# Convolution with 2x2 max pool on one core: the differences of four steps made in two halves, and all instructions in a new order

## The chip, the core and the metric

The kernel runs on one core of a Trainium2 chip. A core has five engines that work at the same time, each through its own queue of instructions: TensorE (PE: matmuls; its weight loads are shown apart as PEld), VectorE (DVE), ScalarE (ACT), GpSimd (POOL) and SyncE (SP, which here only issues transfers). Matmuls write into PSUM, a memory of eight banks. The metric is the time of one execution on the device in microseconds; lower is better.

## The reference: what is computed

A 3x3 convolution with padding 1 over 16 images of 64 channels and 64x64 points, to 128 channels, and then the maximum over every 2x2 square:

```python
x_pad = np.pad(x, ((0, 0), (0, 0), (pad, pad), (pad, pad)))
conv[b, co] += weight[co, ci, kh, kw] * x_pad[b, ci, kh:kh+h, kw:kw+w]    # over ci, kh, kw
output[b, c, i, j] = np.max(conv[b, c, 2*i:2*i+2, 2*j:2*j+2])
```

Input, weights and output are fp32: x is 16 x 64 x 64 x 64, the weights are 128 x 64 x 3 x 3, the output is 16 x 128 x 32 x 32.

## The kernel before, in words

Two images lie side by side on the 128 partitions (64 channels each); a matmul of one image uses 64 rows of TensorE's array, so that those of the two images ("lane" 0 and 1) can run beside each other. The work is cut into 32 steps: 8 pairs of images times 4 quarters, each quarter 8 output rows, that is 16 rows of the convolution. For each step and lane two PSUM banks are built: A and B stand for the two rows of the convolution under each output row. The larger of both, and then of neighbouring columns, is the output.

There are two kinds of steps, in the sequence `SEQ`. A **K step** (8 of them) multiplies the bf16 rows `kx` themselves. A **W step** (24 of them) first forms sums and differences of fp32 rows `wx` and so needs four products of three taps instead of six for two rows of the convolution. With x0 to x3 for the four rows that an output row needs:

- `E` (tile `we`): x1 - x2, and `S` (tile `ws`): x1 + x2, 512 elements per partition each;
- `V` (tile `wv`): differences of rows two apart, 1024 elements: its even rows serve bank A, its odd rows bank B. Step 1 makes the two halves apart, `Ve` (even rows) and `Vo` (odd rows), into tiles `vh` of 512 elements (`rv_half`).

The products of a W step are P2 (E times the weights GM, begins bank A), P0 (even half of V, into A), P3 (odd half of V, into B) and P1 (S times GP, into B). Those of a K step are PAa and PAb into A, PBa and PBb into B, and PR with `KS`, the sum of two rows of `kx`. Products of both lanes that stand next to each other in the order are issued tap by tap in turn. Around the products stand, for each step `s` and lane `l`:

- `SE.s.l` (`seed`, on ScalarE, L439) or `SEv.s.l` (on VectorE, L437): copies A, with P2 alone in it, to bank B. It comes between P2 and P0, and P0 and P3 wait for it. Where bank B held transposed weights, `seed` first issues a matmul of zeros into it;
- `EV` (ScalarE, L423 and L425): copies A out to the tile `ev`; `MX` (VectorE, L443): maximum of B and `ev`, into B. P1 or PR, which is common to both rows, is added behind it;
- `OD` (ScalarE, L466) copies the odd columns, `CM` (VectorE, L475) takes the maximum with the even ones, `ST` stores two lanes of a step. With `CM` the bank is free for another step.

`CP` (ScalarE, L290) lifts the row x1 into a PSUM bank for some steps, and `E` and `S` on VectorE then read it there (L294). All other row operations on VectorE and POOL go through `row_op` (L196). There a POOL operation is made to wait for the last VectorE row operation, or cast by VectorE (L193), that stands ahead of it in the order; lifted E and S do not count:

```python
inst = eng[e].tensor_tensor(out=out, in0=in0, in1=in1, op=op)
if e == "g":
    behind(inst, last_row[0])
else:
    last_row[0] = inst
```

Loads: `LX` (SP's queue) brings a chunk of `wx`, or of the fp32 `kf` of steps 0 and 2, which `XO` and `XE` cast to odd and even rows of `kx`; `LK` (POOL's queue) loads `kx` with a cast on the way. A load waits for the outputs of the step 12 (W) or 13 (K) ahead of it. At the start the weights are combined (`c.`), transposed on TensorE into PSUM banks (`T.`) and copied out (`TV.`, L240 to L244).

The order of all this is written out by hand, as a list of tokens in `ORDER`: each engine executes its own tokens in the order of the list. `:v`, `:a` and `:g` say VectorE, ScalarE and POOL; a number says a PSUM bank; a letter behind the lane (`1a`) means half of the rows. Tiles come from pools with a fixed number of buffers, in the order of the list: 8 for each of `ks`, `ws` and `we`, 6 for `wv`, 4 for `vh`.

Of the kernel before, what the change touches and what calls it, by code (L numbers as in the profile page):

```python
# [20 lines left out]
PAa.0.1b PAa.0.0b EV.1.0 MX.1.1 E.3:v PAb.0.0a PAb.0.1a MX.1.0 PBb.0.1a PBa.0.0b PAb.0.1b PAb.0.0b  # L21
XE.2:a S.3:v PBa.0.1b PBb.0.0a XO.2:a EV.0.0 P2.3.0:5 P1.1.1 KS.0:v EV.0.1 SE.3.0:2 E.4:v OD.1.1
PBb.0.0b PBb.0.1b LX.6 PAa.2.1:0 P1.1.0 OD.1.0 MX.0.1 LK.5 MX.0.0 P0.3.0 PBa.2.1:3 EV.3.0 P3.3.0
PR.0.1 LX.7 OD.0.1 CM.1.1 CM.1.0 LK.9 PAb.2.1 PR.0.0 LX.8 CP.6:5 P2.3.1:7 PAa.2.0:6 MX.3.0 CM.0.1
PBb.2.1 P1.3.0 V.4:g EV.2.1 SE.3.1:4 E.6:v OD.0.0 S.6:v PAb.2.0 P2.4.1:0 P2.4.0:5 P3.3.1 S.4:g
KS.2:v OD.3.0 LX.10 CM.3.0 LX.11 EV.2.0 SE.4.1:6 CM.0.0 PBa.2.0:2 P0.3.1 LX.13 LX.12 E.7:g PBb.2.0
P0.4.1 MX.2.1 SE.4.0:1 P0.4.0 PR.2.1 V.6:v EV.3.1 MX.2.0 P2.6.1:7 P3.4.0 EV.4.1 PR.2.0 P3.4.1 MX.3.1
EV.4.0 OD.2.1 LK.14 MX.4.0 V.7:g SE.6.1:5 CM.2.1 PAa.5.0:0 P1.3.1 OD.2.0 OD.3.1 CM.2.0 MX.4.1 P1.4.0
P0.6.1 P3.6.1 PBa.5.0:3 CM.3.1 PAb.5.0 PAa.5.1:2 OD.4.0 P1.4.1 P2.6.0:4 EV.6.1 V.10:g CM.4.0 PAb.5.1
PBb.5.0 CP.8:1 S.7:g EV.5.0 MX.6.1 OD.4.1 E.8:v S.8:v P2.7.0:7 P1.6.1 SE.6.0:0 EV.5.1 OD.6.1 CM.4.1  # L30
SE.7.0:6 PBa.5.1:1 P0.6.0 MX.5.0 EV.6.0 E.10:g P3.6.0 P2.7.1:2 CM.6.1 KS.5:v P0.7.0 PBb.5.1 SE.7.1:5
EV.7.0 PR.5.0 P2.10.1:4 S.10:v P0.7.1 P3.7.0 OD.5.0 MX.6.0 MX.5.1 SE.10.1:7 LX.16 CM.5.0 P1.6.0
P3.7.1 MX.7.0 PR.5.1 PAa.9.0:3 EV.7.1 OD.6.0 V.8:g LX.15 OD.5.1 CM.6.0 P2.8.0:2 P0.10.1 MX.7.1
CM.5.1 PAb.9.0 P3.10.1 CP.11:0 E.11:v ST.0 P1.7.1 P1.7.0 EV.10.1 SE.8.0:1 EV.9.0 S.11:v V.13:g
OD.7.1 P0.8.0 P2.8.1:4 ST.4 OD.7.0 MX.10.1 ST.6 CM.7.1 P2.10.0:3 PAa.9.1:0 P3.8.0 P1.10.1 CM.7.0
EV.8.0 SE.8.1:5 SE.10.0:2 PAb.9.1 PAa.14.0:6 OD.10.1 E.12:g P0.8.1 P0.10.0 V.11:v KS.9:v EV.9.1
EV.8.1 P3.10.0 P3.8.1 EV.10.0 CM.10.1 PAa.14.1:0 PAb.14.0 MX.8.0 MX.8.1 ST.2 LX.17 PBa.9.0:7
PBa.9.1:4 ST.5 MX.10.0 PAb.14.1 P1.8.0 V.12:g ST.3 CP.13:3 E.13:v EV.14.0 P2.11.1:6 P1.10.0 LK.18
KS.14:v OD.8.0 EV.14.1 PBb.9.0 P1.8.1 S.13:v V.16:g OD.10.0 P2.11.0:0 PBb.9.1 SE.11.1:3 OD.8.1
# [44 lines left out]
def kernel(  # L84
# [9 lines left out]
    BF16 = mybir.dt.bfloat16  # L94
    MAX = mybir.AluOpType.max
    ADD = mybir.AluOpType.add
    SUB = mybir.AluOpType.subtract

    B, CI, H, W = x.shape
# [229 lines left out]
        t = row["E", s] = row_pool.tile([128, R, W], BF16, name="we")  # L329
        two_rows(s, t, e, SUB)  # L330

    def rv(s, e):
# [36 lines left out]
    def pw(block, name, first, stride=1, at=0):  # L369
        def of(s, l, part):  # L370
            half = (name + "eo"[at], s)
            t, n, f = (row[half], 1, 0) if half in row else (row[name, s], stride, at)
            i0, i1 = PARTS[part]
            return (
                block, i0, i1,
                lambda lo, c0, c1: t[lo : lo + CI, f + n * i0 : n * i1 : n, c0:c1],
                first,
            )

        return of  # L380
# [135 lines left out]
    for token in ORDER.split():  # L516
# [29 lines left out]
            lift(int(args[0]), int(at))  # L546
        elif name in ("XO", "XE"):
            to_bf16(int(args[0].rstrip("ab")), args[0].lstrip("0123456789"), int(name == "XO"), at)
        elif name in ("KS", "S", "E", "V"):
            f = rs_cast if name == "S" and int(args[0]) in ADDED else None  # L550
            (f or {"KS": ks, "S": rs, "E": re, "V": rv}[name])(int(args[0]), at)
# [54 lines left out]
```

## Time and profile before

| | |
|---|---|
| median of 3 runs | 104.32 us (103.85 to 105.15) |
| the profiled execution | 103.82 us, of which the span is 102.1 us |
| busy TensorE, VectorE, ScalarE, POOL | 95.8, 91.3, 89.4, 80.2 us |
| read from and written to HBM | 17.07 MB and 8.39 MB, 249 GB/s over the span |

The span runs from the first instruction to the last that the profiler recorded; the rest of the execution's time, 1.7 us, lies around it. A row of the groups reads: line, engine, operation, output tile, input tiles, shapes, count, busy us, mean ns of one, and the idle time of the engine just ahead with what ended it. A row of the timeline begins with its start and its length in us; several equal instructions in a row are one row with a count, and its length is then from the first start to the last end.

### The profile page before, as it was taken

How to read it: one execution, taken by the hardware profiler on the slowest of the kernel's cores; microseconds unless marked ns; L12 is line 12 of the kernel's file. 1: busy time of each engine (PE TensorE's matmuls, PEld its weight loads, DVE VectorE, ACT ScalarE, POOL GpSimd, SP SyncE). 2: the span in 40 equal slices, each digit the busy share in tenths (PEclk: the TensorE clock that was granted, in tenths of full speed). 3: DMA queues.
4: the chain of work that ended last, by engine and by line, in shares of the span. 5: the costliest groups of instructions: out<-in, count | busy, mean ns of one | idle time of the engine just before them, and what ended most of it. 6: DMA issues, size and time to landing. Idle time of an engine off the chain costs nothing.

```text
span 102.1 us, 2473 instructions
## 1 busy us (share of the span) xinstructions
PE 95.8 (94%) x869; PEld 56.0 (55%) x869; DVE 91.3 (89%) x178; ACT 89.4 (88%) x199; POOL 80.2 (79%) x63
## 2 busy tenths in 40 slices
PE   6968999999999999999999999999999999999940
PEld 2335844677785466444787655555555555564610
DVE  0599999999999999999989998699998999988980
ACT  5589989979989998999899988999998987999830
POOL 7006997799699397999899999998698999999000
PEclk9999999999999999999999999999999999999995
DMA  2999999993279999567897999968998505302353
GB/s 64 307 265 417 424 409 326 302 345 70 84 171 387 303 348 358 108 87 175 185 361 196 305 310 367 307 233 180 334 371 291 206 6 206 103 12 94 116 198 103
DMA packets 13789, 24.07 MB, mean 236 GB/s; under 512 B 1104, under 2 KB 9680, under 8 KB 13776
## 3 DMA queue, kind: packets, MB, share of 16 engines
q1 hardware_dynamic: 12624, 22.16, 65.3%
q0 software_dynamic: 864, 1.56, 8.9%
q10 hardware_dynamic: 288, 0.20, 0.6%
q8 instruction: 7, 0.11, 0.5%
q14 instruction: 6, 0.05, 0.1%
HBM read 17.07 MB, written 8.39 MB: 249 GB/s over the span
## 4 chain that ended last, share of the span: by engine, by line
PE 86%; DVE 5%; DMA 4%; ACT 1%; issue 0%; SPq 0%; DVEq 0%
PE acc L408 86%; DMA wx<-in_x_dram 4%; DVE o L475 1%; DVE acc L443 1%; DVE we L196 1%; ACT od L466 1%; DVE acc L437 1%; DVE vh L196 1%; DVE wq L196 1%; SPq L536 0%; DVE o L485 0%; DVE ws L196 0%; DVEq L443 0%
## 5 line engine op out<-in xcount | busy, mean ns | idle before, releaser
L408 PEld LDWEIGHTS <-wt 64*128 64x128 bf16 x840 | 53.8, 94 | 37.6 <-ACT acc L439 2.6
L408 PE MATMUL acc<-wv,wt 64*128 64x504 bf16 (+1 forms) x276 | 58.5, 377 | 0.0
L196 POOL TENSOR_TENSOR wv<-wx 128x1024 bf16<-128x1024 f32 x21 | 49.4, 2359 | 5.5 <-DVE ks L196 2.1
L443 DVE TENSOR_TENSOR acc<-acc,ev 128x512 f32<-128x512 f32 x64 | 43.2, 692 | 2.8 <-ACT ev L423 1.9
L408 PE MATMUL acc<-kx,wt 64*128 64x504 bf16 (+5 forms) x216 | 38.2, 350 | 0.0
L408 PE MATMUL acc<-we,wt 64*128 64x512 bf16 (+1 forms) x144 | 36.6, 377 | 1.0 <-ACT wt L240 0.9
L408 PE MATMUL acc<-ws,wt 64*128 64x512 bf16 (+1 forms) x144 | 34.6, 377 | 0.2 <-DVE acc L443 0.2
L423 ACT ACTIVATE ev<-acc 128x512 f32<-128x512 f32 x48 | 28.8, 608 | 1.2 <-PE acc L408 0.9
L439 ACT COPY acc<-acc 128x512 f32<-128x512 f32 x46 | 27.2, 595 | 1.4 <-DVE o L475 0.4
L475 DVE TENSOR_TENSOR o<-acc,od 128x256 f32<-128x256 f32 x64 | 25.4, 414 | 1.7 <-ACT od L466 0.9
L466 ACT COPY od<-acc 128x256 f32<-128x256 f32 x64 | 23.4, 382 | 3.2 <-PE acc L408 1.9
L196 POOL TENSOR_TENSOR we<-wx 128x512 bf16<-128x512 f32 x11 | 14.0, 1268 | 2.1 <-PE acc L408 1.4
L408 PE MATMUL acc<-ks,wt 64*128 64x504 bf16 (+1 forms) x48 | 12.4, 376 | 0.0
L196 POOL TENSOR_TENSOR ws<-wx 128x512 bf16<-128x512 f32 x9 | 11.4, 1266 | 0.4 <-DVE ks L196 0.4
L425 ACT COPY ev<-acc 128x512 f32<-128x512 f32 x16 | 9.3, 589 | 1.2 <-PE acc L408 1.1
L294 DVE TENSOR_TENSOR we<-acc,wx 128x512 bf16<-128x512 f32 x11 | 7.5, 682 | 0.0
L294 DVE TENSOR_TENSOR ws<-acc,wx 128x512 bf16<-128x512 f32 x11 | 7.5, 681 | 0.0
L290 ACT COPY acc<-wx 128x512 f32<-128x512 f32 x11 | 6.6, 599 | 0.1
L196 POOL TENSOR_TENSOR vh<-wx 128x512 bf16<-128x512 f32 x1 | 1.3, 1277 | 5.2 <-DVE vh L196 5.2
L503 PE MATMUL acc<-const-bfloat16-1.0 128*128 128x512 bf16 x8 | 3.6, 627 | 0.8 <-PEq L587 0.8
L196 DVE TENSOR_TENSOR gsum<-wraw 128x192 f32<-128x192 f32 x1 | 0.5, 502 | 3.6 <-DMA wraw<-in_weight_dram 3.6
L275 POOL DMA_DIRECT2D kx<-in_x_dram x6 | 3.5, 586 | 0.2 <-issue 0.2
(29 smaller groups left out, 32.1 us busy)
## 6 DMA issues: line engine op xcount, KB each, us to landing
out_dram<-o SPq DMA_DIRECT2D x30, 256.0 KB, 6.0
wx<-in_x_dram SPq DMA_DIRECT2D x12, 512.0 KB, 6.8
wx<-in_x_dram SPq DMA_DIRECT2D x6, 544.0 KB, 6.0
wx<-in_x_dram SPq DMA_DIRECT2D x6, 480.0 KB, 7.9
kx<-in_x_dram POOLq DMA_DIRECT2D x3, 256.0 KB, 5.3
kf<-in_x_dram SPq DMA_DIRECT2D x1, 512.0 KB, 7.8
kx<-in_x_dram POOLq DMA_DIRECT2D x2, 240.0 KB, 8.7
wraw<-in_weight_dram SPq DMA_DIRECT2D x1, 288.0 KB, 2.8
```

Source lines behind the costliest of these rows:

```text
L196: inst = eng[e].tensor_tensor(out=out, in0=in0, in1=in1, op=op)
L275: paced(s, nc.gpsimd.dma_start(out=kx_of(p)[:, lo:hi, :], in_=rows_of(p, lo, hi)))
L290: nc.scalar.copy(out=acc[bank], in_=wrow(s, 0))
L294: nc.vector.tensor_tensor(out=t, in0=lifted[s], in1=wrow(s, 1), op=op)
L408: yield lambda kw=kw, o0=o0, o1=o1, c0=c0, c1=c1: nc.tensor.matmul(acc[t][:, i0:i1, o0:o1], wt[l * CI : l * CI + CI, K * BLOCKS[block] + T ...
L423: inst = nc.scalar.mul(t, acc[bank["A", s, l]], -1.0)
L425: inst = nc.scalar.copy(out=t, in_=acc[bank["A", s, l]])
L439: nc.scalar.copy(out=acc[b], in_=acc[bank["A", s, l]])
L443: nc.vector.tensor_tensor(out=t, in0=t, in1=ev[s, l], op=MAX)
L466: nc.scalar.copy(out=od[s, l][:, i0:i1], in_=acc[bank["B", s, l]][:, i0:i1, 1::2])
L475: done[s, l] = nc.vector.tensor_tensor(out=outs(s)[:, l, i0:i1], in0=acc[bank["B", s, l]][:, i0:i1, 0::2], in1=od[s, l][:, i0:i1], op=MAX,)
L503: nc.tensor.matmul(acc[n], ones[:, 0:128], ones, start=True, stop=True, skip_group_check=True)
```

## The change

Steps 3, 4, 30 and 31 make their V in two halves, `Ve` and `Vo`, into two tiles `vh`, as step 1 did, instead of one `wv`. Their even halves are on POOL; the odd half of step 3 is on VectorE, the others on POOL. So P0 of these steps can begin when the even half is there, and P3 when the odd half is.

The whole list `ORDER` is replaced, with other banks, and some operations change their engine:

- VectorE no longer has E.4, TV.D2, TV.GP, SEv.1.1, SEv.31.1 and V.11. It has E.7, S.16, Vo.1, Vo.3, XO.0a, XO.0b, SEv.21.1, SEv.25.0 and SEv.31.0 in addition.
- POOL no longer has E.7, S.16, Vo.1 and the four whole V; it has E.4, V.11 and seven halves.
- ScalarE no longer has SE.21.1, SE.25.0, SE.31.0, XO.0a and XO.0b; it has SE.1.1, SE.31.1, TV.D2 and TV.GP.
- SE.1.1 now goes to bank 2, which held transposed weights, so that `seed` issues one matmul of zeros.
- Loads and stores stand in another order: LX.8 ahead of LX.7, LX.13 behind LX.16 and LX.15, LK.5 ahead of the first row operation of POOL.

The beginning, from before and after:

```diff
-LW c.g1:a LX.1 LX.0a T.G1:0 c.GS:v c.g0:a c.D0:v c.GM:v T.D0:1 c.D2:v T.G0:2 c.g2:a T.GM:3 E.1:v
-c.GP:v Ve.1:v TV.GM:a P2.1.1:4 P2.1.0:5 TV.D0:a TV.G1:a TV.G0:a SE.1.0:6 SEv.1.1:7 T.D2:3 T.GP:1
-T.G2:0 P0.1.1 P0.1.0 TV.G2:v Vo.1:g LX.0b XE.0a:a LX.3 XO.0a:a TV.D2:v LX.2 P3.1.1 P3.1.0 S.1:v
-XO.0b:a XE.0b:a V.3:g EV.1.1 LX.4 CP.3:0 TV.GP:v PAa.0.0a:2 PAa.0.1a:3 PBa.0.1a:4 PBa.0.0a:1
...
+LW c.GS:v c.D2:v c.GM:v c.g1:a T.G1:0 T.D2:1 LX.1 c.D0:v c.g2:a E.1:v c.g0:a T.GM:2 TV.G1:a c.GP:v
+T.G0:3 Ve.1:v T.D0:4 LX.0a TV.GM:a TV.G0:a TV.D0:a P2.1.1:5 P2.1.0:6 TV.D2:a SE.1.0:7 XO.0a:v T.G2:0
+TV.G2:v SE.1.1:2 T.GP:3 Vo.1:v LX.0b PAa.0.1a:4 PAa.0.0a:1 XE.0a:a P0.1.0 P0.1.1 XO.0b:v S.1:v
+PBa.0.0a:0 PAb.0.1a LX.3 P3.1.1 P3.1.0 TV.GP:a XE.0b:a LX.2 LX.4 PBa.0.0b PBa.0.1a:3 LX.6 EV.1.0
+LK.5 PAb.0.0a PAa.0.1b EV.1.1 PBb.0.0a PBb.0.1a Vo.3:v KS.0:v MX.1.0 CP.3:6 PBa.0.1b PAa.0.0b Ve.3:g
...
```

The order of VectorE's and POOL's tokens around the places that the prediction names, in the new list (other engines left out):

```
VectorE: XO.0a TV.G2 Vo.1 XO.0b S.1 Vo.3 KS.0 MX.1.0 MX.1.1 E.3 S.3 MX.0.1 MX.0.0 CM.1.0 CM.1.1 E.6 S.6 KS.2
         CM.0.1 CM.0.0 MX.2.1 V.6 MX.2.0 MX.3.1 MX.3.0 CM.2.1 CM.2.0 MX.4.0 CM.3.1 CM.3.0 E.7 MX.4.1 ...
POOL:    LK.5 Ve.3 E.4 S.4 Ve.4 Vo.4 LK.9 LK.14 S.7 V.7 V.10 E.10 V.8 V.11 LK.18 E.12 V.12 E.15 V.13 V.15 E.16
         LK.23 V.16 S.15 E.19 V.17 S.19 V.22 LK.27 V.19 E.21 V.20 V.21 S.21 E.24 V.24 E.26 V.25 V.26 E.29 S.26
         S.29 V.28 V.29 Ve.30 Ve.31 Vo.30 E.31 Vo.31 S.31
```

Six lines of code are new: a token `E.<step>a` or `E.<step>b` for half of the rows of an E, which the new list does not use, and `first and part != "b"` for it in `pw`. Behind them all line numbers are 6 higher (matmuls L408 become L414, `MX` L443 becomes L449).

More of the change, by code (lines that the diff above doesn't have):

```diff
@@ L22 @@
[L22 to L27, printed above, removed]
@@ L330, in re, with re_half @@
         two_rows(s, t, e, SUB)
+    def re_half(s, part, e):
+        if part == "a":
+            row["E", s] = row_pool.tile([128, R, W], BF16, name="we")
+        i0, i1 = PARTS[part]
+        row_op(e, row["E", s][:, i0:i1], wrow(s, 0)[:, i0:i1], wrow(s, 1)[:, i0:i1], SUB)
     def rv(s, e):
@@ L376, in of @@
                 lambda lo, c0, c1: t[lo : lo + CI, f + n * i0 : n * i1 : n, c0:c1],
-                first,
+                first and part != "b",
             )
@@ L548 @@
             to_bf16(int(args[0].rstrip("ab")), args[0].lstrip("0123456789"), int(name == "XO"), at)
+        elif name == "E" and not args[0].isdigit():
+            re_half(int(args[0][:-1]), args[0][-1], at)
         elif name in ("KS", "S", "E", "V"):
```

111 lines of the change are left out of this document (58 added, 53 removed).

## The prediction

> **What bounds the kernel now.** I read the page first (busy shares, chain), then the chain in order of time, then the timeline.
>
> ```profile
> span 102.1 us, 2473 instructions
> ...
> PE 95.8 (94%) x869; PEld 56.0 (55%) x869; DVE 91.3 (89%) x178; ACT 89.4 (88%) x199; POOL 80.2 (79%) x63
> ...
> PE acc L408 86%; DMA wx<-in_x_dram 4%; DVE o L475 1%; DVE acc L443 1%; DVE we L196 1%; ACT od L466 1%; DVE acc L437 1%; DVE vh L196 1%; DVE wq L196 1%; SPq L536 0%; DVE o L485 0%; DVE ws L196 0%; DVEq L443 0%
> ```
>
> TensorE is the bound: 86% of the chain that ended last is its matmuls. But VectorE and ScalarE, at 89% and 88% busy, are close behind. The chain in order of time (start us, length us, what) says where TensorE was held up:
>
> ```profile
> 8.20 24.43 PE acc L408 x246
> ...
> 43.14 0.29 DVE ws L196
> ...
> 43.82 52.16 PE acc L408 x471
> ...
> 96.07 0.71 DVE acc L443
> ```
>
> After 8.20 us the chain leaves TensorE for VectorE's operations at 43.1 and again at the end. To make a scale of this I need the price of TensorE's unit of work. A product (three taps) of one lane runs beside one of the other lane; three such pairs start at 14.16, 14.81 and 15.46, and the last product of the kernel at 97.42:
>
> ```profile
> 14.16 0.38 PE L408 MATMUL acc<-wv,wt 64*128 64x512 bf16 x1
> ...
> 14.81 0.38 PE L408 MATMUL acc<-kx,wt 64*128 64x512 bf16 x1
> ...
> 15.46 0.38 PE L408 MATMUL acc<-we,wt 64*128 64x512 bf16 x1
> ...
> 21.45 0.38 PE L408 MATMUL acc<-ws,wt 64*128 64x512 bf16 x1
> ...
> 97.42 0.31 PEld L408 LDWEIGHTS <-wt 64*128 64x128 bf16 x2 [0.28 <-issue]
> ```
>
> A pair costs 0.65 us. Both orders hold 136 pairs (840 matmuls). From 8.20 to 97.42 lie 134 of them, 134 x 0.65 = 87.1 us, in 89.2 us. **All that TensorE loses to waits after its start is 2.1 us**: some 0.8 of it around the last products, 1.3 spread before. A new order can win little more than that, and the end stays: in both orders P0.31, EV.31, MX.31 and P1.31 hang on each other in this way with only P1.30 beside them. Two products of one lane follow each other at 79 places before and 69 after, of little weight.
>
> Which engine is nearest to holding TensorE up (busy us of PE, PEld, DVE, ACT, POOL in 8 us; then clock, DMA):
>
> ```profile
> 16.00:24.00 8.00, 8.00 (x77) 5.04 (x73) 8.00 (x17) 7.22 (x17) 6.58 (x5) 1.00 1.02 294
> ...
> 64.00:72.00 8.00, 8.00 (x78) 4.09 (x74) 6.89 (x15) 7.97 (x20) 6.99 (x4) 1.00 0.83 235
> ```
>
> From 16 to 24 us VectorE has no idle time; from 64 to 72 it has 1.1 us. What the change puts on VectorE early is what can cost. The granted clock is full.
>
> **The change, part by part.** VectorE's prices, from start to start:
>
> ```profile
> 11.67 0.68 DVE L294 TENSOR_TENSOR ws<-acc,wx 128x512 bf16<-128x512 f32 x1
> 12.26 0.41 DVE L196 TENSOR_TENSOR ks<-kx 128x512 bf16<-128x512 bf16 x1
> 12.60 0.68 DVE L196 TENSOR_TENSOR we<-wx 128x512 bf16<-128x512 f32 x1
> 13.20 1.29 DVE L443 TENSOR_TENSOR acc<-acc,ev 128x512 f32<-128x512 f32 x2
> 14.40 0.74 DVE L475 TENSOR_TENSOR o<-acc,od 128x256 f32<-128x256 f32 x2
> ...
> 18.81 1.25 DVE L196 TENSOR_TENSOR wv<-wx 128x1024 bf16<-128x1024 f32 x1
> 19.99 1.88 DVE L443 TENSOR_TENSOR acc<-acc,ev 128x512 f32<-128x512 f32 x3
> ```
>
> That is 0.60 for 512 elements in fp32, 0.34 for a KS or a CM, 1.18 for a V. POOL's:
>
> ```profile
> L196 POOL TENSOR_TENSOR wv<-wx 128x1024 bf16<-128x1024 f32 x21 | 49.4, 2359 | 5.5 <-DVE ks L196 2.1 <-DVE ws L196 1.2 <-DMA wx<-in_x_dram 0.8
> ...
> L196 POOL TENSOR_TENSOR we<-wx 128x512 bf16<-128x512 f32 x11 | 14.0, 1268 | 2.1 <-PE acc L408 1.4 <-DVE ks L196 0.8
> ...
> L275 POOL DMA_DIRECT2D kx<-in_x_dram x6 | 3.5, 586 | 0.2 <-issue 0.2
> ```
>
> *Splitting.* Two halves on POOL, priced like the we, cost 2 x 1.27 = 2.54 for 2.36: 0.18 more for each of steps 4, 30 and 31. Step 3's odd half goes to VectorE.
>
> *Balance of engines.* VectorE gives up E.4, the weight copies TV.D2 and TV.GP, the seeds SEv.1.1 and SEv.31.1 and V.11 (0.60 + 0.6 + 1.2 + 1.18 = 3.6). It takes E.7, S.16, Vo.1, Vo.3, three seeds (21.1, 25.0, 31.0) and the two casts XO.0 (4 x 0.60 + 1.8 + 0.67 = 4.9): **+1.3 us**. Such a cast is on no row of VectorE. The nearest rows are the CM of 0.34, with as many elements, and the ws of 0.86 at 8.58 (below); I take the CM's, and a gain below it is not excluded. POOL gives up E.7, S.16, Vo.1 and four V (3 x 1.27 + 4 x 2.36 = 13.2) and takes E.4, V.11 and seven halves (8 x 1.27 + 2.36 = 12.5): -0.7. ScalarE drops three seeds and two casts for two seeds and two weight copies: about -0.4.
>
> [...]
>
> *The start.*
>
> ```profile
> 5.71 0.69 DVE L196 TENSOR_TENSOR we<-wx 128x512 bf16<-128x512 f32 x1
> ...
> 6.46 0.82 PE L408 MATMUL acc<-we,wt 64*128 64x512 bf16 x6 [0.90 <-ACT wt L240]
> ...
> 6.85 0.69 DVE L196 TENSOR_TENSOR vh<-wx 128x512 bf16<-128x512 f32 x1
> ...
> 7.33 0.57 ACT L439 COPY acc<-acc 128x512 f32<-128x512 f32 x1
> ...
> 7.62 1.28 POOL L196 TENSOR_TENSOR vh<-wx 128x512 bf16<-128x512 f32 x1 [5.19 <-DVE vh L196]
> 7.82 1.37 ACT L191 CAST kx<-kf 128x320 bf16<-128x320 f32 x4
> ...
> 8.58 0.86 DVE L196 TENSOR_TENSOR ws<-wx 128x512 bf16<-128x512 f32 x1
> ...
> 9.59 2.40 PE L408 MATMUL acc<-kx,wt 64*128 64x256 bf16 x42
> ```
>
> P2.1 begins at 6.46, right behind E.1 (5.71 + 0.69), which stays fifth on VectorE: no change. Then ScalarE makes both seeds: the second from 7.82 to 8.39, so P0.1 of lane 1 begins at 8.44 instead of 8.20 (+0.24). Ahead of it TensorE now does a half pair of step 0 (six matmuls, 6 x 2.40/42 = 0.34): its rows are cast from 7.45 to 7.8 and it runs from 7.95 to 8.29, inside that wait. Net **-0.1**. With a cast of 0.86 the cover is gone and 0.4 is lost instead. The seed of 1.1 now meets a bank that held transposes, which adds a matmul of zeros; at the 0.38 of a 512-column matmul, or at nearly twice that, it lies in the same wait.
>
> *The first third.* VectorE's own queue, from Ve.1 at 6.85 to the end of MX.3.1: 15 instructions of 0.60 (Ve.1, Vo.1, S.1, Vo.3, E.3, S.3, E.6, S.6, seven MX; S.1 without the stretch of the 0.86, since POOL is then idle), six of 0.335 (two XO, four CM), two KS, TV.G2 for 0.3, V.6 for 1.18: 9.0 + 2.0 + 0.7 + 0.3 + 1.2 = 13.2. That ends at 20.0, and 0.1 later its result is out. TensorE wants it for P1.3.1, 17.4 pairs behind P0.1: 8.44 + 17.4 x 0.65 = 19.75. So it **waits 0.35**. In the old order the product at 21.45 stands 20 pairs behind 8.20, due at 21.2: 0.25 lost by then. The difference is +0.1 if VectorE never idles. Behind MX.3.1 stand MX.3.0 and two CM, wanted just as early; I add 0.1.
>
> *The middle.* A row operation of VectorE and one of POOL do not run side by side:
>
> ```profile
> 41.62 1.26 POOL L196 TENSOR_TENSOR we<-wx 128x512 bf16<-128x512 f32 x1
> ...
> 42.49 0.94 DVE L196 TENSOR_TENSOR ws<-wx 128x512 bf16<-128x512 f32 x1
> ...
> 43.61 2.35 POOL L196 TENSOR_TENSOR wv<-wx 128x1024 bf16<-128x1024 f32 x1 [0.21 <-DVE ws L196]
> ```
>
> This ws took 0.94 instead of 0.68, and POOL's we ended at 42.88, between; it is the piece at 43.14 in the chain. The 0.86 at 8.58 is the same beside POOL's vh, which ended at 8.90. The new order sets E.7, KS.14, KS.9, S.12, KS.18 and S.16 close behind a POOL operation; KS.18 behind V.15, a full 2.36. By the balance above VectorE is then some 0.5 us less ahead of TensorE than it was. The cost lies between 0 (POOL always done) and 1.9 (a whole V less that 0.5); I take **0.3**, nearest to the 0.26 of this row.
>
> [...]
>
> *The last third.* POOL now runs from V.16 to V.24 without a pause: seven V, six E or S and one load's issue, 7 x 2.31 + 6 x 1.24 + 0.57 = 24.2 (starts lie 0.04 closer than the durations say: two wv take 4.67).
>
> ```profile
> 20.16 4.67 POOL L196 TENSOR_TENSOR wv<-wx 128x1024 bf16<-128x1024 f32 x2 [0.67 <-DVE wv L196]
> ...
> 68.64 2.35 POOL L196 TENSOR_TENSOR wv<-wx 128x1024 bf16<-128x1024 f32 x1
> ...
> 72.18 1.02 PE L408 MATMUL acc<-wv,wt 64*128 64x512 bf16 x7
> ```
>
> Begun behind S.16 at pair 60, at 8.44 + 58.5 x 0.65 + 0.4 = 46.9, it has V.24 ready at 71.1. TensorE wants it one pair earlier than at the old 72.18, and with the 0.4 lost by then at 71.9: 0.8 of cover, where the old order had 1.2 (71.0 to 72.18). Costed at nothing; beyond 0.8 it costs one for one. SP's queue moves LX.13 behind LX.16 and LX.15, which wait for the outputs of steps 4 and 3, with 17 pairs (11 us) left to its first use:
>
> ```profile
> wx<-in_x_dram SPq DMA_DIRECT2D x6, 480.0 KB, 7.9
> ```
>
> A load lands 7.9 us after issue at the slowest of its medians, so it stays hidden. LK.5 now stands ahead of all POOL work and issues about 2 us earlier.
>
> **Sum.** -0.1 + 0.1 + 0.1 + 0.3 = +0.4 us on the profiled execution's 103.82 (span 102.1 and 1.72 around it): 104.2. That execution is 0.5 below the median of the runs, 104.32; on the median, **104.7**.
>
> **The rivals.** *The spread losses go* (103.3): of the 1.3 us before the end a third stays. For it: S stands 13 pairs ahead of its P1 in the median instead of 10, so fewer row operations are urgent. Against: a seed stands 1.0 pair ahead of its P0 instead of 1.5, and VectorE gets more work. *Nothing moves* (104.3): splitting does nothing, as no V was late before, and the waits change places. [...] *All losses go, those of the end too* (102.2).
>
> **Chances.** Forecast 0.37 (104.4 to 105.6), nothing moves 0.17, spread losses go 0.26, collisions 0.16, all losses go 0.04. Two per cent, 2.1 us, is about what a measurement of this kernel can tell from no change: faster by more 0.04, slower by more (over 106.4) 0.16, within 0.80. The range, 103.0 to 106.8, takes in the rival of the spread losses and reaches to the price of the collisions; what lies beyond is left out with the last rival. Casts at 0.86 (+0.5 at the start, once more on VectorE's queue) end inside it.
>
> **What would show it.** P0.1 near 8.4 behind a zeros matmul and a half pair of kx; VectorE without a gap until 24 us and TensorE waiting for an MX (now L449) near 20; a KS longer than 0.41 near 44; V.24 done near 71; the same end. The forecast is too low if VectorE idles early, and too high if its row operations show no stretch and TensorE's losses before the end fall below 0.6 us.

## The result, and the profile after

| | before | after |
|---|---|---|
| median of 20 runs each | 104.03 us (103.66 to 105.15) | 103.68 us (103.24 to 105.46) |
| ratio, 95% interval | | 0.9951 (0.9929 to 0.9973) |
| the profiled execution; its span | 103.82; 102.1 us | 103.85; 102.1 us |
| busy TensorE, VectorE, ScalarE, POOL | 95.8, 91.3, 89.4, 80.2 us | 96.1, 91.5, 89.4, 79.4 us |

The kernel became faster by 0.5%, where a time 0.4 us longer was forecast: the time lies inside the stated range, but it moved the other way. Ratios, here and below, leave out the runs that were over 1.5% slower than the fastest of their kernel; medians and ranges hold all runs. The two profiled executions have equal spans, which by itself says nothing of the change. In the after-profile E.1 began 0.23 us later than in the one of before (5.94 against 5.71), because the first load landed later (5.92 against 5.69); the old kernel's own E.1 began at 6.16 in another execution.

The page of after, its head, busy shares and chain by line:

```profile
span 102.1 us, 2485 instructions
...
PE 96.1 (94%) x870; PEld 54.7 (54%) x870; DVE 91.5 (90%) x181; ACT 89.4 (88%) x198; POOL 79.4 (78%) x65
...
PE acc L414 86%; DMA kf<-in_x_dram 6%; DVE o L481 1%; DVE acc L449 1%; ACT od L472 1%; ACT acc L445 1%; SPq L262 0%; SPq L542 0%; DVE o L491 0%; DVE kx L193 0%; DVEq L449 0%; ACTq L290 0%
```

Busy times and shares hardly moved. The chain in order of time (start, length, what) says where it now leaves TensorE:

```profile
8.40 44.19 PE acc L414 x422
...
52.62 0.02 ACT od L472
...
52.89 0.60 ACT acc L445
...
53.53 42.46 PE acc L414 x388
...
96.09 0.71 DVE acc L449
```

The old chain left TensorE at 43.1 for VectorE. This is gone; the new one leaves it at 52.6 for ScalarE. The end is the same. To see how much each place is worth, one compares products that stand at the same place of TensorE's queue in both orders: the first pair behind the seeds, the pair of P3.4.0 (18 pairs later), the pair of P1.13.1 (pair 61), the pair of PBb.18.1 (pair 79) and P1.31.1. Their rows in the timeline of before (the first and the last, at 8.20 and 97.42, stand in the prediction):

```profile
20.15 0.38 PE L408 MATMUL acc<-we,wt 64*128 64x512 bf16 x1
...
47.97 0.38 PE L408 MATMUL acc<-ws,wt 64*128 64x512 bf16 x1
...
59.78 0.38 PE L408 MATMUL acc<-kx,wt 64*128 64x512 bf16 x1
```

and in that of after, with E.1 ahead of them:

```profile
5.94 0.69 DVE L196 TENSOR_TENSOR we<-wx 128x512 bf16<-128x512 f32 x1
...
8.40 0.50 PE L414 MATMUL acc<-kx,wt 64*128 64x256 bf16 x6 [0.24 <-DVE kx L193]
...
20.65 0.38 PE L414 MATMUL acc<-vh,wt 64*128 64x512 bf16 x1
...
47.74 0.38 PE L414 MATMUL acc<-ws,wt 64*128 64x512 bf16 x1
...
60.03 0.38 PE L414 MATMUL acc<-kx,wt 64*128 64x512 bf16 x1
...
97.44 0.09 PEld L414 LDWEIGHTS <-wt 64*128 64x128 bf16 x1 [0.28 <-issue]
```

Where the two products of a pair begin apart, the row is that of the later one. The differences of these starts, with the terms of the prediction's sum:

| stretch | before | after | difference | predicted |
|---|---|---|---|---|
| E.1 to the first pair | 2.49 | 2.46 | -0.03 | -0.1 |
| to pair 19 | 11.95 | 12.25 | +0.30 | +0.2 |
| to pair 61 | 27.82 | 27.09 | **-0.73** | **+0.3** |
| to pair 79 | 11.81 | 12.29 | **+0.48** | 0 |
| to the last product | 37.64 | 37.41 | -0.23 | 0 |
| sum | | | -0.21 | +0.4 |

From pair 19 on, these stretches hardly vary from one execution to the next: another trace of before has 27.83 to pair 61 and 11.81 to pair 79, two more of after have 27.11 and 27.10, 12.30 and 12.29. The first third varies more (11.95 and 12.03 in before, 12.25, 12.23 and 12.20 in after). So the table is a firmer reading than the two spans. The sum is -0.21 us in this pair of traces; the ratio of the runs says -0.5 us (0.3 to 0.7).

A part of the gap between the two can lie in the first stretch, which is the least steady. It was 2.46, 2.50 and 2.31 in the three traces of after, and 2.16 to 2.71 in five of the kernels below that begin as after does; it was 2.49 in both traces of before, and 2.47 to 3.28 in its variants. The rest of the gap is not located.

### The profile page after: what moved, and what is told of

Read it like the earlier page. It is cut to its first block, busy times and chain, and to the rows that moved or that the text cites. A ratio compares the mean times of both kernels' runs of the same rounds, so it can differ in the third digit from the quotient of the medians.

```text
span 102.1 us, 2485 instructions
## 1 busy us (share of the span) xinstructions
PE 96.1 (94%) x870; PEld 54.7 (54%) x870; DVE 91.5 (90%) x181; ACT 89.4 (88%) x198; POOL 79.4 (78%) x65
## 4 chain that ended last, share of the span: by engine, by line
PE 86%; DMA 6%; DVE 2%; ACT 1%; SPq 1%; issue 1%; DVEq 0%; ACTq 0%
PE acc L414 86%; DMA kf<-in_x_dram 6%; DVE o L481 1%; DVE acc L449 1%; ACT od L472 1%; ACT acc L445 1%; SPq L262 0%; SPq L542 0%; DVE o L491 0%; DVE kx L193 0%; DVEq L449 0%; ACTq L290 0%
## 5 line engine op out<-in xcount | busy, mean ns | idle before, releaser
L414 PEld LDWEIGHTS <-wt 64*128 64x128 bf16 x840 | 52.3, 94 | 38.5 <-issue 2.8
L414 PE MATMUL acc<-wv,wt 64*128 64x504 bf16 (+1 forms) x228 | 49.4, 377 | 0.3 <-ACT acc L445 0.3
L449 DVE TENSOR_TENSOR acc<-acc,ev 128x512 f32<-128x512 f32 x64 | 42.9, 691 | 2.0 <-ACT ev L429 1.1
L196 POOL TENSOR_TENSOR wv<-wx 128x1024 bf16<-128x1024 f32 x18 | 42.2, 2355 | 2.6 <-DVE ks L196 1.6
L414 PE MATMUL acc<-kx,wt 64*128 64x504 bf16 (+6 forms) x216 | 38.9, 350 | 0.2 <-DVE kx L193 0.2
L414 PE MATMUL acc<-we,wt 64*128 64x512 bf16 (+1 forms) x144 | 35.0, 377 | 0.5 <-DVE we L196 0.5
L414 PE MATMUL acc<-ws,wt 64*128 64x512 bf16 (+1 forms) x144 | 35.1, 377 | 0.2 <-DVE acc L449 0.2
L445 ACT COPY acc<-acc 128x512 f32<-128x512 f32 x45 | 26.3, 587 | 2.2 <-PE acc L414 0.5
L414 PE MATMUL acc<-ks,wt 64*128 64x504 bf16 (+1 forms) x48 | 12.6, 377 | 0.0
L414 PE MATMUL acc<-vh,wt 64*128 64x504 bf16 (+1 forms) x60 | 10.2, 377 | 0.0
L196 POOL TENSOR_TENSOR ws<-wx 128x512 bf16<-128x512 f32 x8 | 10.1, 1266 | 0.1
L196 POOL TENSOR_TENSOR vh<-wx 128x512 bf16<-128x512 f32 x7 | 8.8, 1269 | 0.6 <-DVE ks L196 0.6
```

The costliest lines, as they stand in the source:

```text
L414: yield lambda kw=kw, o0=o0, o1=o1, c0=c0, c1=c1: nc.tensor.matmul(acc[t][:, i0:i1, o0:o1], wt[l * CI : l * CI + CI, K * BLOCKS[block] + T ...
L445: nc.scalar.copy(out=acc[b], in_=acc[bank["A", s, l]])
L449: nc.vector.tensor_tensor(out=t, in0=t, in1=ev[s, l], op=MAX)
```

## The experiments

The numbers in the text are medians and ratios to the kernel before, with the 95% interval where the runs give one. Stretches are those of the table above, read at the same products.

### Both kernels again

No edit.

> The changed kernel once more, for a second trace. Theory A (order): the old order loses about 0.75 us of TensorE time between 33 and 50 us, the new one almost none, which pays for the 0.45 us it loses before 21 us; the ratio stays near 0.995 and the second trace again shows no TensorE loss between 22 and 50 us. In the first trace the first load of wx landed 0.23 us later and the first kf load 0.9 us later than in the old kernel's trace. Theory B (loads): that is chance, and with early loads the span falls to about 101.7 us, where the middle is unchanged. If the late loads belong to the new order, E.1 starts at 5.9 us again.

Measured: 103.81 us, 0.9951 (0.9918 to 0.9984); stretches 12.23, 27.11, 12.30.

> The changed kernel, a third trace. Its first two had the first kf load at 8.03 and 8.06 us, the traces of the old kernel and its variants at 7.12 to 7.46. If that is chance, a third trace may show it near 7.3, and then TensorE stands 0.2 to 0.3 us earlier at pair 13 (7.5 to 7.6 us above the pairs' own time instead of 7.88) and the span is 101.5 to 101.8 us. If it is at 8.0 again, something in the new kernel delays it.

Measured: one execution, 104.27 us, span 102.5; stretches 12.20, 27.10, 12.29.

> The old kernel, a second trace of the unchanged file. TensorE's losses between pairs 37 and 61 should be 0.74 us again, with the waits at 43.8, 47.3 and 48 us; the kf load lands between 7.1 and 8.1 us if that is chance.

Measured: one execution, 104.38 us, span 102.6; stretches 12.03, 27.83, 11.81. In these three traces E.1 began at 5.93, 6.50 and 6.16 us; its load ended 0.75 us of VectorE's idle time in the second and landed at 6.14 in the third. So the 0.5% repeats, and what differs between these executions of one kernel is mostly the start.

### The splitting alone, in the old order

```diff
-V.3:g ... V.4:g ... V.30:g ... V.31:g
+Ve.3:g Vo.3:g ... Ve.4:g Vo.4:g ... Ve.30:g Vo.30:g ... Ve.31:g Vo.31:g
```

> The old order with the four V made in two halves on POOL, one behind the other in the same place. POOL does 4 x 0.18 = 0.7 us more work, and P0 and P3 of these steps wait for 1.27 us less or 0.18 us more. POOL was not what TensorE waited for, so I expect a ratio of 1.000 (within 0.003); if the halves themselves bring the gain, 0.995.

Measured: 104.41 us, 1.0034 (1.0003 to 1.0066); stretches 11.90, 27.83, 11.82, and 37.65 to the last product, as in before. Halves put in the place of the four V bring nothing: none of these V was late in the old order.

### The splitting taken out of the new order

```diff
-Vo.3:v KS.0:v ... Ve.3:g ... Ve.4:g ... Vo.4:g ... Ve.30:g ... Ve.31:g ... Vo.30:g ... Vo.31:g
+KS.0:v ... V.3:g ... V.4:g ... V.30:g ... V.31:g
```

> The new order with the four steps' differences whole again: V.3 and V.4 on POOL where their even halves stood, V.30 at Ve.30 and V.31 at Vo.31; Vo.3 is gone from VectorE, which gets 0.60 us. If the halves themselves bring the gain, the ratio to the old kernel goes to 1.000 or above. If the order of the rest brings it, the ratio stays at or below 0.995; with the 0.60 us on VectorE it may reach 0.991.

Measured: 105.61 us, 1.0131 (1.0092 to 1.0170), 1.8% above after. This edit does two things: it makes the four V whole, and it puts all of step 3's V on POOL. (The profiled execution took 107.13 us, more than the median, so single operations alone are read from it; its stretches behind pair 61 are those of after all the same, 12.29 and 37.45, and so show no cost of the whole V.30 and V.31.)

### The odd half of step 3 on POOL

```diff
-Vo.3:v KS.0:v ... Ve.3:g
+KS.0:v ... Ve.3:g Vo.3:g
```

> Step 3's odd half Vo.3 goes from VectorE to POOL, directly behind Ve.3. VectorE's gapless queue of the first 24 us is 0.60 us shorter ahead of S.6, MX.2.0 and MX.3.1. If that queue is what costs TensorE its waits of 0.25, 0.23, 0.15 and 0.10 us at 17.2 to 20.6 us, they shrink to under 0.3 us in all, and, where nothing later takes it back, the kernel is 0.3 to 0.5 us faster than the changed one (ratio to the old kernel about 0.991). Rival: ScalarE's seeds or the PSUM banks hold TensorE there; then the waits stay and the ratio stays at 0.995.

Measured: 104.77 us, 1.0057 (1.0033 to 1.0080), 1.1% above after. The first third lengthened from 12.25 to 13.44. Here the V are still in halves; the unsplit kernel, with the same work on POOL, is a further 0.7% slower.

The timelines of the last two kernels and of after say what happened at the same place. After, POOL's Ve.4 and VectorE's KS.2:

```profile
15.10 1.29 POOL L196 TENSOR_TENSOR vh<-wx 128x512 bf16<-128x512 f32 x1
...
16.43 0.41 DVE L196 TENSOR_TENSOR ks<-kx 128x512 bf16<-128x512 bf16 x1
```

With Vo.3 on POOL, S.4 is still running when KS.2 comes, and Ve.4 follows it, 0.97 later than in after:

```profile
14.83 1.28 POOL L196 TENSOR_TENSOR ws<-wx 128x512 bf16<-128x512 f32 x1
...
15.86 1.75 DVE L196 TENSOR_TENSOR ks<-kx 128x512 bf16<-128x512 bf16 x1
...
16.07 1.26 POOL L196 TENSOR_TENSOR vh<-wx 128x512 bf16<-128x512 f32 x1
...
18.66 0.61 PE L414 MATMUL acc<-vh,wt 64*128 64x512 bf16 x4 [1.05 <-ACT acc L445]
```

Unsplit, a whole V.4 stands there (in that one execution):

```profile
15.78 2.68 DVE L196 TENSOR_TENSOR ks<-kx 128x512 bf16<-128x512 bf16 x1
...
15.84 2.33 POOL L196 TENSOR_TENSOR wv<-wx 128x1024 bf16<-128x1024 f32 x1
```

The KS that takes 0.41 us alone took 1.75 where a half came next on POOL and 2.68 where a whole V did. By its record it began while POOL's S.4 still ran, and POOL's next operation, which followed S.4 without a gap, seems to have got in ahead of it: KS.2 ends 0.28 and 0.29 us behind that one, so it did its work after POOL's end. So this late KS.2 lost time to two of POOL's operations in a row. A half in the place of a whole V made the KS 0.93 us shorter here. In the new order KS.2 begins 0.04 us behind the end of POOL's half: it pays nothing, but has no reserve.

### Row operations of POOL displaced

```diff
-Vo.3:v ... S.4:g Ve.4:g ... KS.2:v ... Vo.4:g ... S.7:g ... E.10:g
+Ve.4:g ... KS.2:v Vo.3:g ... Vo.4:g S.4:g ... E.10:g S.7:g
```

> Vo.3 goes to POOL again, but behind KS.2 and Ve.4, so that Ve.4 is not delayed; S.4 goes behind Vo.4 and S.7 behind E.10. VectorE's queue ahead of S.6 and MX.3.1 is 0.60 us shorter, POOL has Ve.4 ready 1.2 us earlier than in the changed kernel. If VectorE's queue is what TensorE waits for between 17 and 21 us, the 0.73 us there fall to 0.2 and the kernel gains 0.4 to 0.5 us on the changed one (ratio about 0.991). If KS.2 or E.7 is blocked by POOL's operations, VectorE loses the 0.60 again and the ratio stays near 0.995 or is worse.

Measured: 106.31 us, 1.0194 (1.0138 to 1.0250); the middle lengthened from 27.09 to 29.63. After has E.7 in the 0.73 us between two V of POOL:

```profile
20.66 2.35 POOL L196 TENSOR_TENSOR wv<-wx 128x1024 bf16<-128x1024 f32 x1
...
22.98 0.68 DVE L196 TENSOR_TENSOR we<-wx 128x512 bf16<-128x512 f32 x1
...
23.74 2.36 POOL L196 TENSOR_TENSOR wv<-wx 128x1024 bf16<-128x1024 f32 x1 [0.73 <-DVE we L196]
```

The displaced order has it in a V, and TensorE waits for what stands behind it on VectorE:

```profile
22.45 2.38 POOL L196 TENSOR_TENSOR wv<-wx 128x1024 bf16<-128x1024 f32 x1
...
23.02 2.37 DVE L196 TENSOR_TENSOR we<-wx 128x512 bf16<-128x512 f32 x1
...
26.05 0.37 PE L414 MATMUL acc<-ws,wt 64*128 64x512 bf16 x1 [1.38 <-DVE acc L449]
```

These are the collisions that the chances name, 2.6 us above after, in an order that lets them happen.

### Two row operations shifted to VectorE, in the old order

```diff
-E.7:g ... CM.4.0 ... S.16:g
+E.7:v CM.4.0 ... S.16:v
```

> The old order with one part of the change alone: E.7 and S.16 on VectorE instead of POOL (E.7 ahead of CM.4.0, S.16 at its place). If this shift between the engines was what took the losses out of the middle, less than 0.4 of the 0.74 us is left there and the time is 0.3 below before. If the place of every operation in the queues did it, VectorE's 1.2 us more cost 0.3 to 0.8 and the losses in the middle grow.

Measured: 106.89 us, 1.0206 (1.0128 to 1.0284). E.7, at the place given to it here, ran into a V again:

```profile
21.40 4.66 POOL L196 TENSOR_TENSOR wv<-wx 128x1024 bf16<-128x1024 f32 x2 [2.62 <-DVE wv L196]
...
24.61 2.00 DVE L196 TENSOR_TENSOR we<-wx 128x512 bf16<-128x512 f32 x1
```

The middle took 29.53, the stretch behind it 12.29 (old 11.81). The three old waits of the middle (below) are all still there, so the shift alone removes nothing, and it costs what its places cost. It was one pair of places; the shift at the new order's places was not tried apart from the rest.

### What held up the old order's middle: single places

```diff
 e6:  -S.12:v CM.9.0
      +CM.9.0 S.12:v
 e9:  the same, and
      -CP.17:3 CM.11.0 ST.11 EV.12.1
      +CM.11.0 ST.11 EV.12.1 CP.17:3
```

> The old order with CM.9.0 ahead of S.12 on VectorE. In the old trace S.12 stretches to 0.94 us beside a POOL operation and CM.9.0 behind it releases the bank that P2.12.1 waits 0.25 us for at 43.8. If the old order's waits of the middle come from this place, TensorE's loss from 37 to 62 pairs falls from 0.75 to 0.5 us or less, and the ratio is about 0.9975. If they are a chain of ScalarE and banks that takes the next free slot, the ratio stays at 1.000 and the wait turns up at 47 us.

Measured: 104.05 us, 0.9989 (0.9950 to 1.0027); middle 27.81.

> The old order with CM.9.0 ahead of S.12 and, on ScalarE, the lift CP.17 behind EV.12.1 as the new order has it. With S.12 moved alone the wait of 0.25 us at 43.8 went and the one of P2.15.1 at 47.2 grew from 0.24 to 0.48: there it waits for the bank that EV.12.1 frees, behind the 0.5 us of CP.17. If this place of ScalarE's queue is what the old order's waits of the middle come from, P2.15.1 waits less than 0.1 us, TensorE loses 0.4 to 0.5 us less by pair 61, and the ratio is about 0.996, that of the changed kernel. If the wait moves on again (to SE.15.1 or P0.17.0), the ratio stays at 1.000.

Measured: 104.82 us, 1.0035 (0.9998 to 1.0071); middle 27.90, and 12.34 to pair 79 instead of 11.81.

In the timeline of before the waits of the middle end with these operations (the S.12 of 42.49 is in the prediction):

```profile
32.00 0.60 ACT L439 COPY acc<-acc 128x512 f32<-128x512 f32 x1
...
32.65 0.11 PEld L408 LDWEIGHTS <-wt 64*128 64x128 bf16 x4 [0.52 <-ACT acc L439]
...
43.35 0.41 DVE L475 TENSOR_TENSOR o<-acc,od 128x256 f32<-128x256 f32 x1
...
45.93 1.26 POOL L196 TENSOR_TENSOR we<-wx 128x512 bf16<-128x512 f32 x1
...
46.66 0.60 ACT L423 ACTIVATE ev<-acc 128x512 f32<-128x512 f32 x1
...
47.30 1.45 PEld L408 LDWEIGHTS <-wt 64*128 64x128 bf16 x16 [0.35 <-ACT ev L423]
```

At 32.6 and 47.3 ScalarE is last (a seed, and an EV that frees a bank), at 43.8 VectorE (CM.9.0 behind S.12). Taking S.12 out of the way removed the wait at 43.8 and left the stretch as long as it was: the next place waited longer.

The reason lies in one more operation, POOL's E.15 (the row at 45.93), which makes the input of P2.15.1 and ended at 47.20, only 0.06 us before EV.12.1. It stands behind V.15, and V.15 had waited for S.12 (the row at 43.61 in the prediction). With CM.9.0 ahead, S.12 ended no earlier than before (43.41 against 43.43), and so neither did E.15 (47.18): P2.15.1 began at 47.23, though EV.12.1 had ended at 46.96. With CP.17 moved as well, E.15 is last again (47.40 against 47.14), so this move could not help.

### What held up the old order's middle: an engine relieved

In steps 8 to 17 the copy EV (ScalarE), the maximum MX (VectorE) or both treat half of the rows and leave the other half out; the order is untouched. Where EV alone is shorter, MX takes its half twice and keeps its length of 0.69 us.

```diff
-inst = nc.scalar.mul(t, acc[bank["A", s, l]], -1.0)
+h = R // 2 if 8 <= s <= 17 else R
+inst = nc.scalar.mul(t[:, 0:h], acc[bank["A", s, l]][:, 0:h], -1.0)
...
-nc.vector.tensor_tensor(out=t, in0=t, in1=ev[s, l], op=MAX)
+nc.vector.tensor_tensor(out=t[:, 0:h], in0=t[:, 0:h], in1=ev[s, l][:, 0:h], op=MAX)
```

> The old order; the copies EV of steps 8 to 17 on ScalarE bring over half of the rows, and MX reads this half twice (the output of these steps is left wrong in the other half). 20 operations of ScalarE lose some 0.27 us each; VectorE's keep their length. Theory 'ScalarE's queue held the old middle up' (seeds and EV end last ahead of three of its waits): of the 0.74 us that TensorE loses between its pairs 19 and 61 less than 0.25 is left, and the time is 0.4 to 0.6 below that of the kernel before. Rival 'VectorE held it up': 0.5 or more is left, and the time falls by less than 0.25. Rival 'one chain through both': about half goes, here and with the shorter MX.

Measured: 103.56 us, 0.9923 (0.9886 to 0.9960); middle 27.54, then 11.67.

> The old order; MX of steps 8 to 17 on VectorE takes the maximum of half of the rows alone (the other half is left out), some 0.27 us less for each of 20 operations; ScalarE's keep their length. Theory 'ScalarE's queue': 0.5 or more of the 0.74 us between pairs 19 and 61 is left, and the time falls by less than 0.25. Rival 'VectorE': less than 0.25 is left, the time falls by 0.4 to 0.6.

Measured: 104.08 us, 0.9983 (0.9936 to 1.0030); middle 27.62, then 11.81.

> The old order with both reliefs: EV and MX of steps 8 to 17 over half of the rows (the other half is left out). The shorter EV alone took 0.27 of the 0.74 us out of the old order's middle (pairs 19 to 61), the shorter MX alone 0.19. Theory 'several waits, each with an engine of its own': the two add up, 0.2 to 0.35 us is left, mostly at P2.15.1 near 47, and the time is near that of the shorter EV alone. Rival 'one chain through both engines': less than 0.1 is left, since neither engine holds the other up any more.

Measured: 103.07 us, 0.9901 (0.9878 to 0.9925); middle 27.11, then 11.67. The ends of its middle:

```profile
20.29 0.38 PE L408 MATMUL acc<-we,wt 64*128 64x512 bf16 x1
...
47.40 0.38 PE L408 MATMUL acc<-ws,wt 64*128 64x512 bf16 x1
```

27.11: the old order with both engines relieved takes just what the new order takes with all of the work (27.09). Relief of ScalarE alone gave 0.28 of the 0.71, of VectorE alone 0.20, of both more than their sum, 0.71. Less than 0.1 is left, as the rival "one chain through both engines" had it; but wait by wait the traces show something else. The loss at a product is its pair's start less that of the pair ahead, beyond the 0.65 us of a pair:

| us lost at | P0.8.0 (32.66) | P2.12.1 (43.82) | P2.15.1 (47.31) |
|---|---|---|---|
| before | 0.19 | 0.25 | 0.23 |
| CM.9.0 ahead of S.12 | 0.19 | 0 | 0.46 |
| the same, and CP.17 later | 0.19 | 0 | 0.47 |
| shorter EV | 0 | 0.24 | 0.17 |
| shorter MX | 0.19 | 0.08 | 0.23 |
| both shorter | 0 | 0 | 0.04 |

The first wait is ScalarE's alone and the second mostly VectorE's. What both reliefs give beyond their sum lies in the third, where P2.15.1 needs two operations that end almost together. With the shorter EV, POOL's E.15 (to 46.98) is last, not EV.12.1 (to 46.83):

```profile
45.72 1.26 POOL L196 TENSOR_TENSOR we<-wx 128x512 bf16<-128x512 f32 x1
...
46.44 0.38 ACT L424 ACTIVATE ev<-acc 128x256 f32<-128x256 f32 x1 [0.18 <-PE acc L408]
...
47.03 0.37 PE L408 MATMUL acc<-we,wt 64*128 64x512 bf16 x1
```

With the shorter MX, EV.12.1 is last (48.17 against 48.12):

```profile
48.22 0.11 PEld L408 LDWEIGHTS <-wt 64*128 64x128 bf16 x4 [0.35 <-ACT ev L423]
```

So the third wait is no chain through ScalarE and VectorE. It has two holders side by side, EV.12.1 on ScalarE and, by way of S.12 and V.15, E.15 on POOL, and relief of one leaves the other.

### The control in the new order

The same shorter EV, in after.

> The new order with the shorter EV of steps 8 to 17 (half of the rows left out). Its middle lost 0.03 us, so nothing is to be had there by either theory; the wait of P0.15 for its seed behind OD.15.1 on ScalarE at 53.5 (0.49 us) falls below 0.25 if ScalarE's queue made it. Time 0.2 to 0.4 below that of the new order if nothing else is late, the same if VectorE's next wait comes in its place.

Measured: 103.54 us, 0.9885 (0.9813 to 0.9957), four runs; the interval takes in the ratio of after, 0.9951. Middle 27.07, nothing to be had, then 12.17 instead of 12.29. The wait at P0.15.0 did not go:

```profile
52.03 0.37 ACT L479 COPY od<-acc 128x256 f32<-128x256 f32 x1 [0.27 <-PE acc L414]
...
52.30 0.59 ACT L447 COPY acc<-acc 128x512 f32<-128x512 f32 x1
```

P0.15.0 began at 52.94, behind that seed, and lost 0.47 us as in after. ScalarE had stood idle for 0.27 us: OD.15.1, ahead of the seed SE.15.0 in its queue, waits for TensorE's P1.15.1. It is the place of OD.15.1 that costs, not ScalarE's load; "ScalarE's queue made it" is right in this narrower sense only.

### The new wait at 53.5 taken away

```diff
 e4:  -OD.15.1 P3.16.0 P2.16.1:1 S.19:g SE.15.0:3 P0.15.0
      +P3.16.0 P2.16.1:1 S.19:g SE.15.0:3 OD.15.1 P0.15.0
 e10: the same, and CM.13.0 ahead of CM.15.1
 e8:  e4 and the displaced row operations together
```

> On ScalarE the seed SE.15.0 goes ahead of OD.15.1. In the changed kernel's traces P0.15.0 waits 0.49 us at 53.5, its one large wait of the middle; the seed begins at 52.89 behind the 0.37 of OD.15.1 though its own product is done near 52.6. If the queue of ScalarE is the cause, the wait falls to about 0.25 us and the kernel is 0.2 to 0.3 us faster than the changed one (ratio about 0.993 to the old kernel). If the seed waits for its PSUM bank instead, nothing moves (0.995).

Measured: 104.02 us, 0.9981 (0.9941 to 1.0022); 12.69 to pair 79 instead of 12.29.

> The changed kernel with SE.15.0 ahead of OD.15.1 on ScalarE, as in the run before, and CM.13.0 ahead of CM.15.1 on VectorE. In the run before VectorE stood 0.30 us in front of CM.15.1, with CM.13.0, which frees a bank for P2.17.1, behind it. If that made the new waits of 0.41, 0.17 and 0.28 us, they go, P0.15.0 keeps its 0.22, and the kernel is 0.2 to 0.3 us faster than the changed one (ratio about 0.9925). If other banks hold P2.17.1, the ratio stays at 0.998.

Measured: 103.91 us, 0.9959 (0.9925 to 0.9992); 12.42 to pair 79.

> The two edits of the changed kernel together: SE.15.0 ahead of OD.15.1, and Vo.3 on POOL behind KS.2. If both waits are what they seem and nothing takes them back later, the gains add: 0.6 to 0.7 us on the changed kernel, ratio about 0.989. If a later place (P0.24, the end) takes it back, the ratio stays between 0.991 and 0.995.

Measured: 106.74 us, 1.0210 (1.0155 to 1.0265).

With the seed first, P0.15.0 loses 0.22 us instead of 0.47, so the place of OD.15.1 did make this wait. But OD.15.1 comes later, VectorE idles for it (0.30 us ahead of CM.15.1), and 0.40 and 0.24 us are lost one and three pairs further on. CM.13.0 ahead of CM.15.1 fills that hole and gives 0.27 us back. Neither beats after measurably. The third kernel is as slow as the displaced order alone.

## Why the prediction was wrong, step by step

**What bounds the kernel: right.** TensorE is still 86% of the chain, and the end is as it was (the last MX at 96.07 before, 96.09 after).

**The start (-0.1): right mechanism, size set by a load.** The matmul of zeros was hidden (it ran at 7.62, before the pair), the half pair came first. In the profiled execution the first half of `kf` landed at 8.03, where before had it at 7.15, so VectorE's cast began at 8.06 and gave back most of the gain (-0.03). Kernels that begin as after does show the same: the first pair followed the start of E.1 by 2.16 us where this load landed 1.49 behind that start (Vo.3 on POOL), by 2.31 at 1.94 (the third trace of after), by 2.50 at 2.13 (the second) and by 2.71 at 2.34 (SE.15.0 ahead of OD.15.1). The cast is 0.29 us long in the record. From start to start, as the prediction prices VectorE's operations, the two casts took 0.21 (8.06 to 8.27) and 0.20 us, well below the 0.34 taken for each.

**The first third (+0.2): right sign, measured +0.30** (0.17 to 0.30 over the traces of both kernels). The sum of VectorE's queue held: the casts were 0.26 us cheaper in all, and other operations as much dearer. In the timeline of after, Ve.1, the cast with its wait, what follows it, a wait of TensorE, the three MX and P1.3.1:

```profile
7.08 0.68 DVE L196 TENSOR_TENSOR vh<-wx 128x512 bf16<-128x512 f32 x1
...
8.06 0.29 DVE L193 CAST kx<-kf 128x256 bf16<-128x256 f32 x1 [0.29 <-DMA kf<-in_x_dram]
...
8.27 0.35 DVE L244 COPY wt<-acc 128x384 bf16<-128x384 bf16 x1
...
16.60 1.73 ACT L445 COPY acc<-acc 128x512 f32<-128x512 f32 x3 [0.16 <-DVE ws L294]
...
17.89 0.33 PEld L414 LDWEIGHTS <-wt 64*128 64x128 bf16 x6 [0.36 <-ACT acc L445]
...
19.26 1.88 DVE L449 TENSOR_TENSOR acc<-acc,ev 128x512 f32<-128x512 f32 x3
...
20.60 0.37 PE L414 MATMUL acc<-ws,wt 64*128 64x512 bf16 x1
```

Begun at 7.08 and with 0.29 of waiting for the load, 13.2 us of work end at 20.57; MX.3.1, the second of the three, ended near 20.54, and P1.3.1 began at 20.60. What the prediction did not see is that the same queue already held TensorE up on the way there, and not at P1.3.1: of the three seeds from 16.60 on, the first two wait for banks that S.6 and then CM.0.1 set free, so P0.3.1 costs 0.24 us at 17.2; PR.2.0, behind MX.2.0, costs 0.15 at 20.0, and smaller waits make up the rest.

**The middle (+0.3): the failed step.** The prediction priced what the new order would add and took the old losses there as staying. Measured was -0.73: the old order lost 0.7 us at three waits between pairs 19 and 61, the new one no more than 0.02 at any product. Two things were wrong in it. First, the price of row operations that meet POOL's. The new order does stretch some row operations, as the profile was to show (a KS longer than 0.41 near 44):

```profile
28.55 2.36 POOL L196 TENSOR_TENSOR wv<-wx 128x1024 bf16<-128x1024 f32 x1 [1.23 <-DVE ks L196]
...
30.59 0.61 DVE L196 TENSOR_TENSOR ks<-kx 128x512 bf16<-128x512 bf16 x1
...
39.96 4.67 POOL L196 TENSOR_TENSOR wv<-wx 128x1024 bf16<-128x1024 f32 x2
...
44.34 0.58 DVE L196 TENSOR_TENSOR ks<-kx 128x512 bf16<-128x512 bf16 x1
```

KS.14 and KS.18 lost 0.20 and 0.17 us, the other four operations that the prediction named kept their length, and TensorE felt nothing of it. Second, and larger, the spread waits of the old order. The prediction gave their end 0.26, arguing against it that a seed stands closer to its P0 and that VectorE gets more work. The first holds for the median alone (the mean is 1.2 pairs in both orders), the second is true, and neither decided. The old waits were three places where an operation came late: one on ScalarE, one on VectorE, and one on ScalarE and POOL together (the table of losses above). In the new order, with more work on VectorE, the same products have what they need in time: SE.8.0 ends 0.38 us before P0.8.0 begins, P2.12.1 and P2.15.1 take banks that were set free 0.15 and 0.19 us before, and E.15 is ready at 39.99 for a P2.15.1 at 46.45. Which of the many moves were needed for it isn't settled: two single moves and the shift of E.7 and S.16 did not do it.

**The last third (0): one wait missed, one gain missed.** The new +0.48 just behind the middle is in the main SE.15.0 behind OD.15.1 (0.47 lost at P0.15.0), a wait that the order itself contains: ScalarE's queue has an operation that needs P1.15.1 ahead of one that P0.15.0 needs, two pairs later. It could have been read from the order. The rest ran 0.23 us shorter than in before; its waits are small, and none was tried. POOL behaved as summed: V.24 was ready at 68.90 + 2.35 = 71.25 (predicted 71.1), and P0.24.1 began at 71.70 with no loss:

```profile
68.90 2.35 POOL L196 TENSOR_TENSOR wv<-wx 128x1024 bf16<-128x1024 f32 x1
```

**Splitting: half right.** That no V was late in the old order is confirmed (halves alone, 1.0034). But halves are not idle in the new order, where they keep POOL's blocks short beside KS.2. Without them, and with all of step 3's V on POOL, the kernel is 1.8% slower than after; 1.1% of this comes with Vo.3 on POOL alone, so the halves themselves account for some 0.7%.

**The rivals.** "The spread losses go" named the right place, and the time fell between it (103.3) and "Nothing moves" (104.3): the middle's losses went, 0.48 came back at a new wait. The collisions (0.16 in the chances) are no phantom: each kernel that set a row operation of VectorE beside one of POOL's (Vo.3 on POOL, unsplit, displaced, shifted) was 1.1 to 2.4% slower than the order that it was made from. The new order avoids them by having row operations of the two engines meet end to start where it matters (KS.2 took 0.41 us there, E.7 0.68). No run shows the price of 106.8 to which the range reaches, an estimate of the author's; the runs took 104.77 us (Vo.3 on POOL), 105.61 (unsplit), 106.31 (displaced) and 106.89 (shifted, in the old order).

## What to carry to other kernels

Before pricing a new order, list the waits of the old one between fixed products and ask of each which operations end last there, and which end just before them; a wait with two holders side by side doesn't yield to a move of one of them, but a new order can take both away. A hand-written order should be read for pairs such as "an operation that waits for TensorE ahead of one that TensorE waits for"; such a wait is visible without a run. Where row operations of two engines hold each other up as they did here, read the sums of both queues to a tenth of a microsecond: E.7, slipped into a V of 2.38 us, took 2.37 us instead of 0.68.

## What the runs showed of the hardware

- The same first loads landed at different times from one execution to the next, in both kernels: the load of E.1 at 5.69 and 6.14 us in two traces of before and at 5.92 in one of after (in another E.1 waited for it until 6.50), the first half of `kf` at 7.15 in before and at 8.03 and 8.06 in two traces of after. A profiled pair is therefore to be compared from a product on, not by its spans.
- From a fixed product to a fixed product, behind the first third, the times repeated within 0.03 us or so (27.82 and 27.83 in the old order, 27.09, 27.11 and 27.10 in the new one), so a stretch between two products tells a tenth of a microsecond, where the intervals of the ratios above reach 0.2 to 0.8% to each side.
- A row operation of VectorE that came while POOL had one running showed as a long operation, not as idle time: KS.2, 0.41 us in after, took 1.75 with Vo.3 on POOL, and E.7, 0.68 in after, took 2.37 in the displaced order.
